# First stage of a hybrid decoder layer in quarters of two feature tiles, with squares summed on TensorE

## The chip, the core and the metric

The kernel runs on one core of one Trainium2 chip. The metric is the device time of one execution in microseconds (us), given as the median of the runs shown. The other engines of the core that matter here are ScalarE (ACT in the profile's rows), VectorE (DVE), GpSimd (POOL) and SyncE (SP), which issues nearly all loads; TensorE is PE, and its weight loads are PEld.

## What is computed

One layer of a decoder for a prompt of 1024 rows and 8 samples of 4 rows, with 1024 features. Everything is float32. What the change touches is the head of the layer: the conditioning vector goes through a silu and a product with `ada_w`, which gives a shift and a scale for each feature; the rows are normalized by their mean square, scaled and shifted, and the result `h` goes through `w_in`.

```python
def _rmsnorm(x, g):
    return x * lax.rsqrt(jnp.mean(x * x, axis=-1, keepdims=True) + EPS) * g

mod = jax.nn.silu(c) @ ada_w + ada_b
sh1, sc1, gt1, sh2, sc2, gt2 = jnp.split(mod[:, None, :], 6, axis=-1)
h = _rmsnorm(x, norm1_g) * (1.0 + sc1) + sh1
u = h @ w_in        # u_x, u_g, u_q, u_k, u_v, u_r, u_lr, u_ga, u_gb
...                 # RG-LRU branch, chunked GLA branch, merge, w_out, SwiGLU FFN
```

## The kernel before

Features lie on the 128 partitions, so the 1024 features are 8 feature tiles, and rows lie along the free dimension. The rows go in two halves: half A is the first 512 prompt rows, half B the other 512 and the 32 sample rows. A runs through the whole layer, then B. Products are made to float32 precision from two-part operands: a weight tile or an `h` tile is split into a high part (a copy by ScalarE, `split_w` line 150, `shift` line 517) and a low part (a subtraction by VectorE, lines 151 and 518), and `gemm` issues three matmuls for a tile: high by high (line 438), high by low (439), low by high (440). Only the third needs the low part of the weight, only the second the low part of `h`.

Only `begin` of half A, lines 549 to 607, is changed, with what it hands on. In it the instructions of TensorE, ScalarE and VectorE stay in the order in which they are written (`as_written`); DMAs go in program order on SP's queue. Its steps are:

- `occupy` (line 1594): dummy matmuls of a mask or a loaded tile into a bank that nobody reads, two passes each, 8 before anything has landed, 4 later.
- `load_x` (line 521): four loads of x, two feature tiles in each. ScalarE squares each tile (lines 468, 471). VectorE adds seven of the squares up into `acc` (line 473); the eighth stays by itself.
- `norm1_sum` (line 532) and `norm` (477): `ssq_mm` (line 443) multiplies 128 rows of a sum by a column of ones, four matmuls for a tile of 512 rows, two tiles in all; `rsqrt` (line 298) is eleven small VectorE instructions; `spread` (line 449) brings the result to all partitions by TensorE and a copy `rb`.
- The conditioning of half of the features (4 tiles) in one piece: chunk 2 is the scale of tiles 0 to 3, chunk 0 the shift of tiles 0 to 3, chunks 3 and 1 the same for tiles 4 to 7. A chunk is four loads of 512 KB, 16 narrow matmuls (`ada_mul`, line 205), a copy of the result by ScalarE (`ada_row`, 211), four transposes and two to three small VectorE instructions (`ada_turn`, 216; `ada_derive`, 246).
- `scaled` (line 542) multiplies x by gain and `rb`, `shift` (line 510) adds the shift and splits into high and low.
- `lr_part` (line 620): a low-rank projection, two matmuls for a feature tile. `part`: the share of a feature tile in four projections, called early (two of q, two of k), which stay in PSUM over the whole stage.

Tiles 0 to 3 are done in this way, then the products of chunks 3 and 1 come in, and parts of tiles 0 to 3 of the third and fourth projection; tiles 4 to 7 of all four and of the low-rank projection are left to `proj_h` (line 640) and `lr` (626), which run in `branches` behind `begin`. There `qk` (line 658) also makes a product `zps` (line 669) between the second and the third early projection. The first instruction after all of that on TensorE is the first matmul of `vps` (values), and from there the order on TensorE is the same in both kernels to the end.

PSUM tiles for the conditioning, the sums and the transposes come from one pool of two banks (`ax`), small float32 tiles from a pool of six (`T`), loads of 512 KB from a pool of 17 (`S`), and the high and low weight tiles from a pool of three.

Of the kernel before, what the change touches and what calls it, by code (L numbers as in the profile page):

```python
# [21 lines left out]
NB = 8  # L22
# [12 lines left out]
def starts_of(w):  # L35
    return [min(i, w - P) for i in range(0, w, P)]
# [7 lines left out]
def bc(ap, shape):  # L44
    return ap.to_broadcast(shape)
# [8 lines left out]
def hybrid_layer(ctx, tc, I, O):  # L54
# [44 lines left out]
    def ax(name):  # L99
        return axp.tile([P, 512], F32, tag="ax", name=name)  # L100
# [110 lines left out]
    def ada_row(cc, ps):  # L211
        row = T(f"adar{cc}")
        act.activation(row[:, :512], ps, AF.Copy)
        return row

    def ada_turn(cc, row):
        tps = ax(f"adat{cc}")
        for i in range(4):
            pe.transpose(tps[:, i * P:(i + 1) * P], row[:, i * P:(i + 1) * P], ident)
        mo = mod[:, 4 * cc:4 * cc + 4, :]  # L220
        dve.tensor_reduce(mo, groups(tps, 9), axis=AX.X, op=OP.add)
        dve.scalar_tensor_tensor(mo, mo, 0.5, bc(vec[:, V_ADAB + 4 * cc:V_ADAB + 4 * cc + 4].unsqueeze(2), [P, 4, 9]),
                                 op0=OP.mult, op1=OP.add)
        ada_derive(cc, mo)
# [21 lines left out]
    def ada_derive(cc, mo):  # L246
        ch, j = cc // 2, 4 * (cc % 2)
        if ch in (1, 4):
            g0 = (V_N1 if ch == 1 else V_N2) + j
            dve.scalar_tensor_tensor(gains[:, ch // 4, j:j + 4, :], mo, 1.0, bc(vec[:, g0:g0 + 4].unsqueeze(2), [P, 4, 9]),  # L250
                                     op0=OP.add, op1=OP.mult)
        if ch in (0, 3):
            sl = shd[:, ch // 3, j:j + 4, :]
            dve.tensor_sub(sl, mo[:, :, 1:9], bc(mo[:, :, 0:1], [P, 4, NB]))
        if ch in (2, 5):
            dve.tensor_scalar_mul(gains[:, 2 if ch == 2 else 3, j:j + 4, :], mo, 0.5)

    ada_next = []

# [52 lines left out]
    def drain(g):  # L312
        for _ in g:
            pass
# [74 lines left out]
    class Half:  # L389
# [159 lines left out]
        def begin(s):  # L549

            begin = len(traced())
            occupy(rmask, 8)
            s.load_x()
            a2, a0 = ada_loads(2), ada_loads(0)
            s.lr_raw = S("lr_raw")[:, :1024]
            sp.dma_start(s.lr_raw, I["w_lr"])
            ts = (T_Q, T_Q + 1, T_K, T_K + 1)
            raws = [load_raw(I["w_in"][t], 1024, f"early{t}") for t in ts[:2]]
            a3, a1 = ada_loads(3), ada_loads(1)
            raws += [load_raw(I["w_in"][t], 1024, f"early{t}") for t in ts[2:]]  # L560
            sums = s.norm1_sum()
            next(sums)
            row = ada_row(2, ada_all(2, a2))
            drain(sums)
            ada_turn(2, row)
            xns = s.scaled(range(4))
            ps = ada_all(0, a0)
            s.lr_weights()
            row = ada_row(0, ps)
            occupy(a0[3], 1)  # L570
            ada_turn(0, row)
            occupy(a0[3], 3)
            s.h = []
# [5 lines left out]
            def part(i, kt):  # L579
                s.gemm(ps[i], hl[i], 1, s.h, kt, kt == 0, False, hk=kt)  # L580

            for kt in range(4):
                s.shift(s.h, xns[kt], s.whole, kt, 0, "1" + s.n)
                if kt == 0:
                    weights(0)
                s.lr_part(kt)
                part(0, kt)
            weights(1)
            for kt in range(4):
                part(1, kt)  # L590
            row3 = ada_row(3, ada_all(3, a3))
            weights(2)
            p1 = ada_all(1, a1)
            ada_turn(3, row3)
            row1 = ada_row(1, p1)
            weights(3)
            xns = s.scaled(range(4, 8))
            for kt in range(4):
                part(2, kt)
                if kt == 1:  # L600
                    ada_turn(1, row1)
            for kt in range(4):
                part(3, kt)
            s.early = {t: (ps[i], hl[i]) for i, t in enumerate(ts)}
            for kt in range(4, 8):
                s.shift(s.h, xns[kt], s.whole, kt, 0, "1" + s.n)
            as_written(begin, (mybir.EngineType.PE, mybir.EngineType.Activation, mybir.EngineType.DVE))


# [16 lines left out]
        def lr(s):  # L626
            n = s.n
            if s.hf:
                s.lr_weights()
            for kt in range(4 * (1 - s.hf), KD):  # L630
                s.lr_part(kt)
# [962 lines left out]
    def occupy(src, n):  # L1594
        for _ in range(n):
            pe.matmul(idle, src[:, :P], src[:, :512], start=True, stop=True, skip_group_check=True)
# [17 lines left out]
    p0, p1 = B.halves  # L1614
# [111 lines left out]
```

## Time and profile before

| | us |
|---|---|
| median of 3 runs | 1978.03 |
| the three runs | 1972.02, 1978.03, 1979.07 |
| the profiled execution: its own time | 1973.25 |
| its span | 1971.5 |
| first matmul on real `h` (low-rank, line 623) | 26.18 |
| first matmul of the values (`vps`) | 59.32 |

The span runs from the first to the last instruction, the time of an execution is 1.75 longer. A timeline row gives the start, the time it took, the engine, the line, the operation, output and inputs, how many such instructions stand together, and in brackets the idle time of the engine ahead of it with what ended it. A float32 matmul of two passes stands there as two instructions. A matmul's time goes from its start to the modelled end of its result, so that matmuls in a row overlap; the step from one to the next is the distance of their starts.

### The profile page before, as it was taken

The numbers are of one execution on the slowest core, as the hardware profiler recorded it, in microseconds if no ns is written. First come the engines' busy times: TensorE is split into PE (matmuls) and PEld (weight loads), VectorE is DVE, ScalarE is ACT, GpSimd is POOL, SyncE is SP. The second block draws the span as 40 slices with busy tenths as digits, with TensorE's granted clock in tenths as the row PEclk, the third lists the DMA queues.
The fourth block names the chain that finished last, engine by engine and source line by source line (L and its number), as shares of the span: only waits on it lengthen the run. The fifth ranks groups of instructions, "written<-read, shape, count | busy, mean of one in ns | idle before, by whom it ended". The sixth has DMA issues, their size and how long they took to land. (4 is left out here: it accounts for less than half of the span.)

```text
span 1971.5 us, 33688 instructions
## 1 busy us (share of the span) xinstructions
PE 1935.8 (98%) x13428; PEld 1761.6 (89%) x13428; DVE 1319.9 (67%) x2293; ACT 944.0 (48%) x1442; POOL 107.7 (5%) x231
## 2 busy tenths in 40 slices
PE   8999999999999999999999999999999999999998
PEld 5877877776899998998899998999999999999997
DVE  5648487655548774677564597684355688888867
ACT  4645475533235452555353355563232344566653
POOL 0000001000000000000000001110222000000000
PEclk9999999999999999999999999999999999999999
DMA  8324235567544467554432323323456544556553
GB/s 339 101 103 166 70 107 200 184 228 258 206 164 155 139 189 249 176 178 141 145 102 69 133 63 100 103 88 107 134 187 223 200 141 126 173 170 183 171 163 109
DMA packets 116798, 307.68 MB, mean 156 GB/s; under 512 B 13729, under 2 KB 28833, under 8 KB 116641
## 3 DMA queue, kind: packets, MB, share of 16 engines
q1 hardware_dynamic: 104656, 260.74, 40.7%
q0 software_dynamic: 11440, 44.23, 6.2%
q8 instruction: 105, 1.72, 0.4%
q10 hardware_dynamic: 544, 0.56, 0.1%
q14 instruction: 53, 0.43, 0.1%
HBM read 271.08 MB, written 34.39 MB: 155 GB/s over the span
## 5 line engine op out<-in xcount | busy, mean ns | idle before, releaser
L151 DVE TENSOR_TENSOR fwa_hl<-fwa,fwa_hl 128x1024 fp32r<-128x1024 f32 (+1 forms) x57 | 68.8, 1206 | 44.7 <-ACT fwa_hl L150 40.8
L151 DVE TENSOR_TENSOR fwb_hl<-fwb,fwb_hl 128x1024 fp32r<-128x1024 f32 (+1 forms) x64 | 77.2, 1206 | 27.8 <-ACT fwb_hl L150 27.0
L150 ACT ACTIVATE fwa_hl<-fwa 128x1024 fp32r<-128x1024 f32 (+1 forms) x57 | 59.3, 1040 | 43.9 <-PE fapsa L1338 10.8
L150 ACT ACTIVATE fwb_hl<-fwb 128x1024 fp32r<-128x1024 f32 (+1 forms) x64 | 66.6, 1041 | 23.5 <-PE fcpsb L1338 9.1
L438 PE MATMUL f3psa<-faa,f3a_hl 128*128 128x512 f32 x176 | 68.6, 390 | 0.6 <-ACT f3a_hl L150 0.6
L440 PE MATMUL f3psa<-faa,f3a_hl 128*128 128x512 f32 x176 | 68.5, 390 | 0.4 <-DVE f3a_hl L151 0.4
L439 PE MATMUL f3psa<-faa,f3a_hl 128*128 128x512 f32 x176 | 68.6, 390 | 0.0
L150 ACT ACTIVATE f3a_hl<-f3a_raw 128x768 fp32r<-128x768 f32 (+1 forms) x32 | 25.3, 792 | 55.7 <-PE f3psa L440 47.4
L438 PE MATMUL uxpsb<-h1b,uxpsb_hl 128*128 128x256 f32 (+1 forms) x160 | 48.1, 300 | 0.1
L439 PE MATMUL uxpsb<-h1b,uxpsb_hl 128*128 128x256 f32 (+1 forms) x160 | 46.8, 292 | 0.0
L440 PE MATMUL uxpsb<-h1b,uxpsb_hl 128*128 128x256 f32 (+1 forms) x160 | 46.3, 290 | 0.0
L438 PE MATMUL ugpsb<-h1b,ugpsb_hl 128*128 128x272 f32 x160 | 46.2, 289 | 0.0
L440 PE MATMUL ugpsb<-h1b,ugpsb_hl 128*128 128x272 f32 x160 | 46.0, 288 | 0.0
L439 PE MATMUL ugpsb<-h1b,ugpsb_hl 128*128 128x272 f32 x160 | 45.8, 286 | 0.0
L438 PEld LDWEIGHTS f3psa<-faa,f3a_hl 128*128 128x128 f32 x176 | 33.0, 188 | 7.7 <-ACT f3a_hl L150 1.0
L440 PEld LDWEIGHTS f3psa<-faa,f3a_hl 128*128 128x128 f32 x176 | 33.0, 188 | 7.7 <-DVE f3a_hl L151 0.9
L151 DVE TENSOR_TENSOR f3a_hl<-f3a_raw,f3a_hl 128x768 fp32r<-128x768 f32 (+1 forms) x32 | 28.2, 888 | 16.8 <-ACT f3a_hl L150 16.6
L439 PEld LDWEIGHTS f3psa<-faa,f3a_hl 128*128 128x128 f32 x176 | 33.0, 188 | 6.8
L438 PE MATMUL wopsb<-mb,wob_hl 128*128 128x272 f32 x128 | 36.9, 289 | 1.1 <-DVE gab L1203 1.1
L438 PE MATMUL rpsb<-h1b,rpsb_hl 128*128 128x272 f32 x128 | 37.8, 295 | 0.0
L438 PE MATMUL vpsb<-h1b,vpsb_hl 128*128 128x272 f32 x128 | 37.4, 292 | 0.0
L439 PE MATMUL rpsb<-h1b,rpsb_hl 128*128 128x272 f32 x128 | 37.4, 292 | 0.0
(1131 smaller groups left out, 7739.7 us busy)
## 6 DMA issues: line engine op xcount, KB each, us to landing
ada<-in_ada_w SPq DMA_DIRECT2D x48, 512.0 KB, 6.2
fwb<-wsum SPq DMA_DIRECT2D x72, 256.0 KB, 3.4
s_raw<-in_ffn SPq DMA_DIRECT2D x32, 512.0 KB, 4.1
wsum<-s_raw POOLq DMA_DIRECT2D x32, 512.0 KB, 3.5
fwa<-wsum SPq DMA_DIRECT2D x64, 256.0 KB, 3.3
fwb<-in_ffn SPq DMA_DIRECT2D x54, 256.0 KB, 3.4
fwa<-in_ffn SPq DMA_DIRECT2D x48, 256.0 KB, 3.2
woa_raw<-in_w_out SPq DMA_DIRECT2D x13, 512.0 KB, 3.3
```

Source lines behind the costliest of these rows:

```text
L150: act.activation(hl[:, 0, :n], raw[:, :n], AF.Copy)
L151: dve.tensor_sub(hl[:, 1, :n], raw[:, :n], hl[:, 0, :n].bitcast(F32))
L438: pe.matmul(out, wh, x[:, o:o + w], start=st, stop=False)
L439: pe.matmul(out, wh, x[:, N + o:N + o + w], start=False, stop=False)
L440: pe.matmul(out, wl, x[:, o:o + w], start=False, stop=en)
```

## The change

`begin` is written anew in four quarters of two feature tiles. The loads of conditioning come in eight pairs (scale of the quarter, then its shift), each quarter's pairs followed by one of the early weights. `products` and `turn` handle half a chunk: 8 matmuls, a copy 256 wide, two transposes, and the small VectorE instructions on two tiles; `ada_derive` takes a start and a length for that. The squares aren't added on VectorE: `ssq_mm` runs on each of the eight squares as it is, 32 matmuls of one column in place of 8, on TensorE behind 5 dummy matmuls in place of 8. In the middle one dummy matmul is left of four. All four early projections and the low-rank projection are finished inside `begin`, so `proj_h` only returns the sums and `lr` has no matmuls left for half A.

```diff
-            occupy(rmask, 8)
-            s.load_x()
+            occupy(rmask, 5)
...
+            for i in range(4):
+                for c, u in cond(i):
+                    loads[c, u] = [ada_load(c, 2 * u + k) for k in range(2)]
+                if i == 0:
+                    s.lr_raw = S("lr_raw")[:, :1024]
+                    sp.dma_start(s.lr_raw, I["w_lr"])
+                raws.append(load_raw(I["w_in"][ts[i]], 1024, f"early{ts[i]}"))
...
+            for kt in range(KD):
+                sq = T(f"sq1{s.n}{kt}")
+                act.activation(sq[:, :N], s.xs[kt], AF.Square)
+                s.ssq_mm(nps, sq, starts, 0, kt == 0, kt == KD - 1)
...
+            products(*sh)
+            scale(0)
+            turn(*sh)
+            occupy(loads[sh][1], 1)
+            s.lr_weights()
+            shift(0)
+            weights(0)
+            low(0)
+            for i in range(1, 4):
+                sc, sh = cond(i)
+                k0, k1 = 2 * i - 2, 2 * i - 1
+                products(*sc)
+                part(0, k0, k1)
+                turn(*sc)
+                scale(i)
+                products(*sh)
+                for e in range(1, i):
+                    part(e, k0, k1)
+                turn(*sh)
+                weights(i)
+                part(i, *range(k1 + 1))
+                shift(i)
+                low(i)
+            for e in range(4):
+                part(e, 6, 7)
...
             if t in s.early:
-                ps, hl = s.early.pop(t)
-                s.gemm(ps, hl, 4, s.h, 4, False, True, hk=4)
-                return ps
+                return s.early.pop(t)
```

**TensorE up to the first matmul on real `h`.** Before, from the eight dummies on (`nps1a` is the sum of squares, `adaps` the products of a chunk, `rps1a` the spread, `adat` the transposes, `lrpsa` the low-rank projection):

```order
L1596 MATMUL idle<-rmask 128x512 x8
L445 MATMUL nps1a<-ones,acc1a 128x1 x4
L445 MATMUL nps1a<-ones,sq1a_181 128x1 x4
L208 MATMUL adaps_248<-ada_183,cth 32x256 x4
L208 MATMUL adaps_248<-ada_185,cth 32x256 x4
L208 MATMUL adaps_248<-ada_187,cth 32x256 x4
L208 MATMUL adaps_248<-ada_189,cth 32x256 x4
L457 MATMUL rps1a<-ident,rstd1a 128x128 x4
L219 MATMUL adat_274<-ident,adar_265 128x128 x4
```

In the changed kernel, from the seventh of eight such sums on (five dummies and six sums of four matmuls stand ahead of it):

```order
L445 MATMUL nps1a<-ones,sq1a_237 128x1 x4
L445 MATMUL nps1a<-ones,sq1a_243 128x1 x4
L584 MATMUL adaps_253<-ada_158,cth 32x256 x4
L584 MATMUL adaps_253<-ada_160,cth 32x256 x4
L592 MATMUL adat_278<-ident,adar_262 128x128 x2
L457 MATMUL rps1a<-ident,rstd1a 128x128 x4
L584 MATMUL adaps_291<-ada_162,cth 32x256 x4
L584 MATMUL adaps_291<-ada_164,cth 32x256 x4
L592 MATMUL adat_306<-ident,adar_300 128x128 x2
L1640 MATMUL idle<-ada_164 128x512
L669 MATMUL lrpsa<-h1a_317,lr_hla 128x512
L670 MATMUL lrpsa<-h1a_317,lr_hla 128x512
```

The sum of squares on TensorE is four times as long, and everything up to the low-rank projection stands behind it.

**VectorE where the second half or quarter of the conditioning arrives.** Before, at the third and fourth early weights (`xn1a` is the scaled x, `h1a` the tile `h`, whose low part is made here):

```order
L221 TENSOR_REDUCE mod<-adat_418 128x36
L222 SCALAR_TENSOR_TENSOR mod<-mod,vec 128x36
L250 SCALAR_TENSOR_TENSOR gains<-mod,vec 128x36
L169 TENSOR_TENSOR early_lo<-early_raw,early_hi 128x1024
L546 SCALAR_TENSOR_TENSOR xn1a_432<-xa_158,gains,rb1a 128x512
```

In the changed kernel, in the second quarter:

```order
L595 TENSOR_REDUCE mod<-adat_347 128x18
L596 SCALAR_TENSOR_TENSOR mod<-mod,vec 128x18
L250 SCALAR_TENSOR_TENSOR gains<-mod,vec 128x18
L546 SCALAR_TENSOR_TENSOR xn1a_353<-xa_152,gains,rb1a 128x512
L546 SCALAR_TENSOR_TENSOR xn1a_355<-xa_152,gains,rb1a 128x512
L595 TENSOR_REDUCE mod<-adat_368 128x18
L596 SCALAR_TENSOR_TENSOR mod<-mod,vec 128x18
L254 TENSOR_TENSOR shd<-mod 128x16
L151 TENSOR_TENSOR early_hl<-early_raw,early_hl 128x1024
L518 SCALAR_TENSOR_TENSOR h1a_383<-xn1a_353,mod,h1a_383 128x512
```

The low part of the quarter's weight (line 151) now stands behind the quarter's shift, which itself waits for transposes on TensorE.

**TensorE at the end of the early projections.** Before (`early_326` to `early_328` are the second to the fourth projection, `zpsa` the product of `qk`):

```order
L440 MATMUL early_326<-h1a_481,early_hl 128x512
L669 MATMUL zpsa_563<-lrta,wa_114 128x512
L669 MATMUL zpsa_566<-lrta,wa_114 128x512
L439 MATMUL early_327<-h1a_472,early_hl 128x512
L440 MATMUL early_327<-h1a_472,early_hl 128x512
```

In the changed kernel:

```order
L439 MATMUL early_252<-h1a_549,early_hi 128x512
L440 MATMUL early_252<-h1a_549,early_lo 128x512
L713 MATMUL zpsa_627<-lrta,wa_114 128x512
L713 MATMUL zpsa_630<-lrta,wa_114 128x512
L438 MATMUL vpsa_644<-h1a_317,vpsa_hl 128x512
```

The product `zps` has moved behind all of the early projections, to directly ahead of the values.

More of the change, by code (lines that the diff above doesn't have):

```diff
@@ L562, in begin @@
[L562 to L573, printed above, removed]
+            N = s.N
+            occupy(rmask, 5)
+            s.xs = []
+            for i in range(4):
+                xt = S(f"x{s.n}{i}")
+                sp.dma_start(xt[:, :2 * N], I["x" + s.n][:, i * 2 * N:(i + 1) * 2 * N])
+                s.xs += [xt[:, :N], xt[:, N:2 * N]]
@@ new lines, in begin @@
+            ts = (T_Q, T_Q + 1, T_K, T_K + 1)
+            cond = lambda i: [(c, i % 2) for c in ((2, 0) if i < 2 else (3, 1))]
+            loads, raws = {}, []
+            for i in range(4):
+                for c, u in cond(i):
[4 more added lines that the diff above has]
+                raws.append(load_raw(I["w_in"][ts[i]], 1024, f"early{ts[i]}"))
@@ new lines, in begin, with products @@
+            starts = starts_of(N)
+            nt = len(starts)
+            nps = ax("nps1" + s.n)
+            for kt in range(KD):
+                sq = T(f"sq1{s.n}{kt}")
+                act.activation(sq[:, :N], s.xs[kt], AF.Square)
+                s.ssq_mm(nps, sq, starts, 0, kt == 0, kt == KD - 1)
+            rows, xns = {}, {}
+            def products(c, u):
+                ps = ax(f"adaps{c}{u}")
+                for k in range(2):
+                    for g in range(4):
+                        pe.matmul(ps[32 * g:32 * g + 32, :256], cth[:, 4 * k + g, :], loads[c, u][k][:, g * 256:(g + 1) * 256],
+                                  start=(k == 0), stop=(k == 1), skip_group_check=True)
+                rows[c, u] = T(f"adar{c}{u}")
+                act.activation(rows[c, u][:, :256], ps[:, :256], AF.Copy)
@@ new lines, in turn @@
+            def turn(c, u):
+                tps = ax(f"adat{c}{u}")
+                for i in range(2):
+                    pe.transpose(tps[:, i * P:(i + 1) * P], rows[c, u][:, i * P:(i + 1) * P], ident)
+                j = 4 * c + 2 * u
+                mo = mod[:, j:j + 2, :]
+                dve.tensor_reduce(mo, groups(tps[:, :256], 9), axis=AX.X, op=OP.add)
+                dve.scalar_tensor_tensor(mo, mo, 0.5, bc(vec[:, V_ADAB + j:V_ADAB + j + 2].unsqueeze(2), [P, 2, 9]),
+                                         op0=OP.mult, op1=OP.add)
+                ada_derive(c, mo, 2 * u, 2)
@@ L574, in begin, with scale @@
+            def scale(i):
+                xns.update(s.scaled((2 * i, 2 * i + 1)))
             hl, ps = [None] * 4, [mm(f"early{t}") for t in ts]
@@ L577, in weights @@
                 hl[i] = (split_w if i < 3 else split_apart)(raws[i], 1024, f"early{ts[i]}")
[L579 to L606, printed above, removed]
+            def part(i, *kts):
+                for kt in kts:
+                    s.gemm(ps[i], hl[i], 1, s.h, kt, kt == 0, kt == KD - 1, hk=kt)
@@ new lines, in shift, with low @@
+            def shift(i):
+                for kt in (2 * i, 2 * i + 1):
+                    s.shift(s.h, xns[kt], s.whole, kt, 0, "1" + s.n)
+            def low(i):
+                for kt in (2 * i, 2 * i + 1):
+                    s.lr_part(kt)
+            (sc, sh) = cond(0)
+            s.h = []
+            products(*sc)
+            rstd = cp.tile([P, 5], F32, name="rstd1" + s.n, tag="rstd", bufs=2)
+            rsqrt(rstd[:, :nt], nps[:, :nt], nt, 1.0 / D, "1" + s.n)
+            turn(*sc)
@@ new lines, in begin @@
+            s.rb1 = [s.spread(rstd[:, :nt], N, "1" + s.n)]
+            products(*sh)
[9 more added lines that the diff above has]
+                k0, k1 = 2 * i - 2, 2 * i - 1
+                products(*sc)
+                part(0, k0, k1)
+                turn(*sc)
+                scale(i)
[7 more added lines that the diff above has]
+                low(i)
@@ L607, in begin @@
+            for e in range(4):
+                part(e, 6, 7)
+            s.early = dict(zip(ts, ps))
             as_written(begin, (mybir.EngineType.PE, mybir.EngineType.Activation, mybir.EngineType.DVE))
@@ L629, in lr @@
                 s.lr_weights()
-            for kt in range(4 * (1 - s.hf), KD):
-                s.lr_part(kt)
+                for kt in range(KD):
+                    s.lr_part(kt)
             ps = s.lr_ps
```

19 lines of the change are left out of this document (6 added, 13 removed).

## The prediction

> **What bounds the kernel now.** I read the page first, then the table of stretches, then the timeline of the beginning, last the granted clock. The page says whose time counts:
>
> ```profile
> span 1971.5 us, 33688 instructions
> PE 1935.8 (98%) x13428; PEld 1761.6 (89%) x13428; DVE 1319.9 (67%) x2293; ACT 944.0 (48%) x1442; POOL 107.7 (5%) x231
> ```
>
> TensorE is the bound; it lacks 35.7 us of the span. The table of stretches, cut at the first matmul on real `h` and at the first of the values, says where:
>
> ```profile
> 0.00:26.15 26.15, 21.06 (x120) 10.86 (x120) 14.70 (x61) 10.47 (x17) 2.32 (x12) 1.00 0.93 353
> 26.15:59.32 33.17, 32.07 (x189) 23.97 (x187) 18.80 (x28) 16.08 (x24) 0.00 (x0) 1.00 0.65 244
> 100.00:440.00 340.00, 339.26 (x1725) 263.84 (x1722) 220.12 (x316) 177.87 (x253) 22.03 (x42) 1.00 0.43 148
> ```
>
> (Length; busy PE, PEld, DVE, ACT, POOL; clock; DMA share; GB/s.) Behind the beginning TensorE is never short of work, 0.74 us in 340. So a microsecond won or lost before the values begin, at 59.32, is one at the end, and the change is worth what it moves that point. The timeline of the first stage:
>
> ```profile
> 12.80 0.95 PE L445 MATMUL nps1a<-ones,acc1a 128*128 128x1 f32 x8
> ...
> 14.57 1.93 PE L208 MATMUL adaps<-ada,cth 128*32 128x256 f32 x32
> 14.68 0.16 DVE L302 TENSOR_SCALAR rs_1a<-nps1a 128x4 f32<-128x4 f32 x1 [2.13 <-PE nps1a L445]
> ...
> 16.65 0.16 DVE L309 SCALAR_TENSOR_TENSOR rstd1a<-rs_1a 128x4 f32<-128x4 f32 x1
> 16.92 1.13 PE L457 MATMUL rps1a<-ident,rstd1a 128*128 128x128 f32 x8 [0.41 <-PE adaps L208]
> 17.88 0.60 PE L219 MATMUL adat<-ident,adar 128*128 128x128 f32 x4
> 18.08 0.60 ACT L460 ACTIVATE rb1a<-rps1a 128x512 f32<-128x512 f32 x1 [0.91 <-PE rps1a L457]
> ...
> 20.57 0.64 PE L208 MATMUL adaps<-ada,cth 128*32 128x256 f32 x8 [0.34 <-DMA ada<-in_ada_w]
> 21.91 1.06 ACT L616 ACTIVATE lr_hla<-lr_raw 128x1024 fp32r<-128x1024 f32 x1 [3.23 <-DMA lr_raw<-in_w_lr]
> 24.00 2.74 PE L1596 MATMUL idle<-ada 128*128 128x512 f32 x6
> 24.77 0.72 ACT L517 ACTIVATE h1a<-xn1a,mod 128x512 fp32r<-128x512 f32 x1 [1.32 <-DVE mod L222]
> 26.18 0.80 PE L623 MATMUL lrpsa<-h1a,lr_hla 128*128 128x512 f32 x1
> ```
>
> The loads end last: shift products wait until 20.57, low-rank weights until 21.91, and `h` follows. The sum of squares was known at 14.6 and its spread at 18.7.
>
> **The change, part by part.** *Loads.* The first shift products need 8 loads of 512 KB where they needed 12. At 353 GB/s or more a load takes 1.3 to 1.5 us (524 KB over that), so they land 5 us earlier, near 15.5. Loads stop being last. For the later quarters the same bytes come in another order: a quarter's five loads take 7 us, less than the 9 to 10 that a quarter will take below. On SP's queue the last load of the fourth quarter's pairs waits for the low-rank weights' buffer, free near 25; behind it stand the fourth early weight and loads for the values, needed far later, so nothing. GpSimd's one load in this stretch has nothing behind it either.
>
> *The sum of squares* is what is late next. VectorE loses six additions, but nobody waited for VectorE there. TensorE gets 64 passes of one column where it had 16. Those 16 took from 12.80 to 14.57, 0.11 each, so 64 take 7.0. They start behind 5 dummies, six passes fewer at 0.43 (six take 2.74, of which the last about 0.6), at 12.8 - 2.6 = 10.2, and end at 17.3, not 14.6. Two squares now wait for a buffer of the six; TensorE comes to them only at 15, so that costs nothing. The root takes 14.68 to 16.81, 2.1: 19.5. The spread and its copy took 1.9: 21.4, not 18.7.
>
> *First shift.* Its products stand behind the spread's passes, from 20.6: 16 passes at 0.05 (31 steps in 1.93 less a last one of 0.38) end at 21.8. A copy of 256 columns is not in the trace; between a small instruction (0.2) and the 512 columns of `rb` (0.60) I take 0.4: 22.2. Two transposes 0.4, the dummy 1.0: 23.6. The low-rank weights take the buffer that this dummy reads, so ScalarE waits for it: 1.06 and 0.7 for the tile make 25.4 for the first real matmul, 0.8 earlier than 26.18.
>
> *The four quarters.* The prices:
>
> ```profile
> 24.20 0.31 DVE L221 TENSOR_REDUCE mod<-adat 128x36 f32<-128x144 f32 x1 [0.91 <-PE adat L219]
> ...
> 24.77 0.19 DVE L254 TENSOR_TENSOR shd<-mod 128x32 f32<-128x32 f32 x1
> 25.40 1.04 ACT L150 ACTIVATE early_hl<-early_raw 128x1024 fp32r<-128x1024 f32 x1
> ...
> 38.35 1.23 DVE L151 TENSOR_TENSOR early_hl<-early_raw,early_hl 128x1024 fp32r<-128x1024 f32 x1 [7.53 <-ACT early_hl L150]
> ...
> 39.63 0.50 PE L440 MATMUL early<-h1a,early_hl 128*128 128x512 f32 x1 [0.37 <-DVE early_hl L151]
> ...
> 59.32 0.39 PE L438 MATMUL vpsa<-h1a,vpsa_hl 128*128 128x512 f32 x1
> ...
> 64.53 0.39 PE L440 MATMUL vpsa<-h1a,vpsa_hl 128*128 128x512 f32 x1
> ```
>
> A wide matmul takes 0.2265 (24 from 59.32 to 64.53, 23 steps). From the first real matmul on TensorE has 112 of them in either kernel, 25.4; narrow passes 64 before, 96 now (5.0); transposes 8, now 12 (1.3); two `zps` 0.45. That is 32.1 of work, where it was 30.1, since half of the first scale and shift no longer lies ahead. Stalls before: 33.1 - 30.1 = 3.0.
>
> Stalls now: in each later quarter the low part of the new weight stands on VectorE behind the shift. After the transposes: 0.2 for their result, 0.7 for three small instructions, 1.23 for the low part, 2.2 in all; TensorE has 0.7 to do meanwhile (a transpose and two matmuls). 1.5 to 1.7, three times. In the second quarter nothing stands between the shift's products and its transposes either, so their copy (0.8) and ScalarE's split of the weight behind it (1.04, of which 0.8 shows) come on top, and the third matmul's wait is 1.2 there. With the ramp of the first two tiles, 0.6 to 0.8, and small change: 0.8 + 2.7 + 1.6 + 1.7 = 6.8. The values begin at 25.4 + 32.1 + 6.8 = 64.3, 5.0 late.
>
> *The product `zps`*, moved behind everything, puts the scores' chain later against the values:
>
> ```profile
> 54.33 1.26 ACT L653 ACTIVATE za<-zpsa,vec 128x512 f32<-128x512 f32 x2
> ...
> 57.71 1.22 DVE L726 SCALAR_TENSOR_TENSOR ea<-za 128x1024 f32<-128x1024 f32 x1
> ...
> 72.69 1.22 DVE L151 TENSOR_TENSOR vpsa_hl<-vpsa_raw,vpsa_hl 128x1024 fp32r<-128x1024 f32 x1
> ...
> 78.80 0.69 PE L830 MATMUL spsa<-wa 128*64 128x64 f32 x16 [0.29 <-ACT vfa L712]
> ```
>
> Its copy ended at 55.6, 3.7 ahead of the values, and will end 1.3 behind: 5.0. Of that the chain waited 2.1 for VectorE (to 57.7), which will be free then, and 1.2 lay in it for a value weight (72.69) that stands ahead now: 5.0 - 2.1 - 1.2 = 1.7 at the scores, which wait already. A copy of k that stood in it on ScalarE (0.6) is done ahead too, which leaves 1.1. Bounds 0 and 3.7, I take 1.2.
>
> *The clock.* One-column passes are the open price: do they keep the clock up? Two places where it fell (the last fence gives the one-column passes `opsb` of its stretch alone):
>
> ```profile
> 445.79:449.21 3.42, 0.00 (x0) 0.00 (x0) 2.87 (x5) 0.00 (x0) 0.53 (x1) 1.00 0.72 277
> 449.21:452.62 3.41, 2.22 (x8) 1.94 (x9) 2.27 (x6) 2.81 (x5) 0.53 (x1) 0.50 0.96 335
> 452.62:456.03 3.41, 3.41 (x15) 1.83 (x13) 1.60 (x5) 1.95 (x2) 0.00 (x0) 0.50 0.96 330
> 456.03:459.44 3.41, 3.41 (x18) 2.71 (x15) 3.41 (x7) 1.34 (x2) 1.33 (x2) 1.00 0.93 292
> ```
>
> ```profile
> 1261.58:1264.99 3.41, 2.92 (x22) 2.67 (x22) 2.60 (x7) 2.27 (x4) 0.00 (x0) 1.00 0.64 222
> 1264.99:1268.40 3.41, 3.41 (x13) 2.95 (x12) 2.68 (x10) 2.21 (x4) 0.00 (x0) 0.50 0.13 39
> ```
>
> ```profile
> 1261.58:1264.99 3.41, 1.98 (x17) 1.81 (x16) 0.17 (x1) 1.00 0.64 222
> ```
>
> It fell to half behind 3.4 us without work, and also behind 3.4 us in which TensorE was busy for 2.92, but 1.98 of that with one-column passes. It came back behind a stretch that was full, not behind one that was 65% full. In the change 10.2 to 17.3 is one-column passes and nothing else, two such stretches long, so wherever the steps of 3.41 lie the clock falls between 13.6 and 17.1. Then passes take double:
>
> ```profile
> 450.40 1.12 PE L219 MATMUL adat<-ident,adar 128*128 128x128 f32 x4 [4.82 <-ACT adar L213]
> ...
> 452.17 0.63 PE L438 MATMUL pbpsa<-yba,pba_hl 128*128 128x512 f32 x1
> ...
> 454.73 0.63 PE L438 MATMUL pbpsa<-yba,pba_hl 128*128 128x512 f32 x1
> ```
>
> (1.12 for the 0.60 of four transposes; wide 0.43, six steps in 2.56.) With a fall at 15.7: the rest of the sum +1.6; spread +0.9, products +0.9, transposes and dummy +1.2. The first real matmul is 4.6 late, at 30. Up to the first full stretch, some 3 to 6 us on, half of the busy time is lost, 1 to 2.5. Together 5.5 to 7, I take 6.0.
>
> The Trainium skill, "TensorE: Matmul & The Clock Gate", section "Why this matters for your kernels", asks only that TensorE have no idle gap over some 3 us between bursts. By that rule the clock would stay up here, for no gap comes near that, and the sum would be 6.2 in place of 12.2. The rows of 1261.58 differ: there TensorE idles 0.49 in all, and the clock falls.
>
> **Sum.** 5.0 + 1.2 + 6.0 = 12.2 us later. The profiled execution took 1973.25, so 1985.5 in its terms. It lies in the low half of the runs shown (1972.02 to 1979.07); the four executions have a mean of 1975.6, and 1975.6 + 12.2 makes 1988. Half a percent, 9.9 us, is about what a measurement of this kernel can tell from no change.
>
> **Rivals.** *The clock stays up*: the sum of squares keeps TensorE busy by the engine's own count, as between 12.3 and 14.6 before, and only stalls and work remain. 5.0 + 1.2 = 6.2, 1982. For it: the clock column is 1.00 through the whole first stage before. Against it: that stretch also held dummies and narrow products.
>
> *The quarters run without a hole*, on the other side: the clock stays up, and TensorE's queue has the row copies and low parts in time, because ScalarE and VectorE are little used there (16.08 and 18.80 of 33.17). The first real matmul at 25.4, 32.1 of work and the first ramp 0.6 make 58.1, 1.2 early; with the scores' chain as before, 1974. It is decided at the third matmul of a quarter's new projection: if the low part is there when TensorE arrives, this holds. Against it: that part is behind the shift in VectorE's order. No more than this can be won: the load, the sum of squares and the work set 58.
>
> *The clock stays down*: every quarter has a stall of over a microsecond, so no stretch is full until the long run of the fourth projection. The second and third quarter then take some 5 us more, 17 in all, 1993.
>
> **How the numbers follow.** Forecast 0.62, the clock stays up 0.20, without a hole 0.08, the clock stays down 0.10. The range takes in the last (1993 and, from the upper runs, 1997) and the lower end of the case with the clock up (6.2 less the 3 that its stalls and the scores are uncertain by, from the mean: 1978; the third reaches lower, and with a part of it I set 1977). Slower by over half a percent: nearly three quarters of the forecast (12.2 with some 3 either way against 9.9) and the whole of the last case, 0.54. Faster by as much would need 9.9 and the bound is 1.2: 0.03, for the measurement. Within: 0.43.
>
> **What would show it.** Right: 64 one-column passes from about 10.2 to beyond 17; the root's first instruction past 17.3; a granted clock of 0.5 from some 15 to past 30; the first real matmul near 30; waits of 1.2 to 1.7 of the third matmul of the second to fourth projection on VectorE's low part; values from 69 to 71; a wait of 1 to 2 at the scores. With the clock at 1.00 throughout, values at 64 and the first rival holds. Values before 60 would make the whole walk wrong; so would a part of the loss given back behind them, in a place where TensorE has idle time now.

## The result, and the profile of the changed kernel

| | before | changed |
|---|---|---|
| median of 7 runs each, us | 1973.68 (1966.12 to 1979.07) | 1985.35 (1983.00 to 1987.26) |
| span of the profiled execution | 1971.5 | 1985.5 |
| first matmul on real `h` | 26.18 | 27.91 |
| first matmul of the values | 59.32 | 70.68 |

The ratio is 1.0055, with a 95% interval from 1.0041 to 1.0069: 8 to 14 us slower, 11 in the middle. The forecast was 12.2 slower, 1988 in a range from 1977 to 1997.

The page of the changed kernel, the same two lines as before:

```profile
span 1985.5 us, 33781 instructions
PE 1944.0 (98%) x13464; PEld 1769.8 (89%) x13464; DVE 1319.5 (66%) x2299; ACT 943.5 (48%) x1446; POOL 108.3 (5%) x231
```

The table of stretches, cut at the same two events (length; busy PE, PEld, DVE, ACT, POOL; granted clock; DMA share; GB/s), and behind the first three rows five steps of 3.41 us:

```profile
0.00:27.91 27.91, 22.18 (x120) 16.00 (x120) 9.55 (x53) 9.35 (x17) 1.76 (x11) 0.82 0.94 352
27.91:70.68 42.77, 37.90 (x222) 25.36 (x223) 21.90 (x41) 15.73 (x25) 0.55 (x1) 0.96 0.45 164
100.00:440.00 340.00, 339.67 (x1737) 263.84 (x1736) 220.63 (x320) 180.42 (x259) 20.72 (x39) 1.00 0.43 145
9.21:12.62 3.41, 3.41 (x32) 3.41 (x33) 0.00 (x0) 2.30 (x4) 0.00 (x0) 1.00 1.03 418
12.62:16.04 3.42, 3.42 (x18) 3.42 (x18) 0.00 (x0) 0.00 (x0) 0.00 (x0) 0.50 1.03 418
19.45:22.86 3.41, 2.85 (x20) 1.89 (x13) 1.82 (x11) 0.38 (x1) 0.00 (x0) 0.50 1.03 410
26.27:29.69 3.42, 1.49 (x4) 0.67 (x4) 1.94 (x4) 3.15 (x4) 0.00 (x0) 1.00 1.02 407
29.69:33.10 3.41, 3.41 (x20) 1.76 (x20) 0.99 (x1) 0.38 (x1) 0.55 (x1) 0.50 1.02 405
```

The first stage is 1.7 us longer, the second 9.6 (42.77 for 33.14). In the 340 us of the third row TensorE idles for 0.33, where it idled for 0.74 before: a wait of 0.5 for a load (`adaps`) is gone, and so little is given back. The clock is 0.82 in the first stage and 0.96 in the second, 1.00 in both before. It is half from 12.62 to 22.86 and again from 29.69 to 33.10. The step ahead of the first fall is the plainest row: TensorE busy for all 3.41 us, 32 passes, and half clock behind it.

The timeline of TensorE up to the first real matmuls, and the places where it waits later:

```profile
8.69 10.06 PE L445 MATMUL nps1a<-ones,sq1a 128*128 128x1 f32 x64
18.67 1.93 PE L584 MATMUL adaps<-ada,cth 128*32 128x256 f32 x16
...
21.65 1.64 PE L457 MATMUL rps1a<-ident,rstd1a 128*128 128x128 f32 x8
23.22 1.07 PE L584 MATMUL adaps<-ada,cth 128*32 128x256 f32 x16
24.85 0.44 PE L592 MATMUL adat<-ident,adar 128*128 128x128 f32 x2 [0.56 <-ACT adar L587]
25.13 1.02 PE L1640 MATMUL idle<-ada 128*128 128x512 f32 x2
27.91 0.49 PE L669 MATMUL lrpsa<-h1a,lr_hla 128*128 128x512 f32 x1 [1.76 <-ACT h1a L517]
...
38.09 0.50 PE L440 MATMUL early<-h1a,early_hl 128*128 128x512 f32 x1 [0.72 <-DVE early_hl L151]
...
47.72 0.50 PE L440 MATMUL early<-h1a,early_hl 128*128 128x512 f32 x1 [1.41 <-DVE early_hl L151]
...
60.11 0.50 PE L440 MATMUL early<-h1a,early_lo 128*128 128x512 f32 x1 [1.44 <-DVE early_lo L169]
...
84.70 0.63 PE L731 MATMUL vtpa<-ident,vfa 128*128 128x128 f32 x4 [1.18 <-DVE atta L801]
```

The sum of squares is one block of 64 passes in 10.06 us and the root starts when it ends. In the first 110 us no matmul waits for a load any more. The third matmul of a new projection waits for VectorE's low part in each later quarter. The last row is a wait that the kernel before did not have: the first transposes of the values, 14 us behind their first matmul.

### The profile page after: what moved, and what is told of

It reads as the page before. It is cut to its first block, busy times and chain, and to the rows that moved or that the text cites. A ratio compares the mean times of both kernels' runs of the same rounds, so it can differ in the third digit from the quotient of the medians.

```text
span 1985.5 us, 33781 instructions
## 1 busy us (share of the span) xinstructions
PE 1944.0 (98%) x13464; PEld 1769.8 (89%) x13464; DVE 1319.5 (66%) x2299; ACT 943.5 (48%) x1446; POOL 108.3 (5%) x231
## 5 line engine op out<-in xcount | busy, mean ns | idle before, releaser
L438 PE MATMUL wopsb<-mb,wob_hl 128*128 128x272 f32 x128 | 37.7, 295 | 2.4 <-DVE gab L1247 2.4
L438 PE MATMUL rpsb<-h1b,rpsb_hl 128*128 128x272 f32 x128 | 37.8, 295 | 0.0
L440 PE MATMUL wopsb<-mb,wob_hl 128*128 128x272 f32 x128 | 37.6, 294 | 0.0
```

What stands on the lines that cost most here:

```text
L438: pe.matmul(out, wh, x[:, o:o + w], start=st, stop=False)
L440: pe.matmul(out, wl, x[:, o:o + w], start=False, stop=en)
```

## The experiments

Eleven kernels were run. "Half clock" is the time up to 100 us in which the trace's clock records show 0.50; the ratio is to the kernel before, run beside them on the same chip (medians of 1971.34, 1972.29 and 1971.61 in the three groups). Line numbers in rows are those of each kernel itself.

| kernel | first real matmul | values | half clock | ratio, 95% interval |
|---|---|---|---|---|
| before | 26.18 | 59.32 | 0 | |
| changed | 27.91 | 70.68 | 13.7 | 1.0055 [1.0041, 1.0069] |
| squares added on VectorE | 23.91 | 65.15 | 3.4 | 1.0049 [1.0032, 1.0065] |
| before, with the tile sums alone | 29.61 | 62.57 | 6.8 | 1.0015 [1.0006, 1.0024] |
| weights first | 28.51 | 65.55 | 10.2 | 1.0047 [1.0032, 1.0061] |
| wide passes between the sums | 32.91 | 76.49 | 17.1 | 1.0080 [1.0067, 1.0094] |
| place of `zps` | 27.89 | 70.43 | 10.2 | 1.0059 [1.0036, 1.0082] |
| three parts put back | 23.72 | 60.77 | 3.4 | 1.0017 [1.0001, 1.0032] |
| sums 64 columns wide | 24.38 | 67.15 | 3.4 | 1.0051 [1.0032, 1.0070] |
| all parts | 22.66 | 61.40 | 6.8 | 1.0002 [0.9988, 1.0016] |
| all parts, three dummies | 22.96 | 59.23 | 0 | 1.0011 [1.0000, 1.0022] |
| wide sums, weights, `zps` | 24.38 | 61.45 | 0 | 1.0009 [0.9996, 1.0023] |
| sums 16 columns wide | 28.22 | 71.02 | 13.7 | one run: 1984.31 us |

The whole times follow the values only roughly. With the squares on VectorE, with the weights first and with the wide sums the values come 5.5, 5.1 and 3.5 us earlier than in the changed kernel, and by the ratios the whole times are 1.2, 1.6 and 0.8 us shorter, with intervals of some 3 us either way. The steps at half clock behind 440 us lie partly elsewhere in their traces; that they make the difference is not shown. So what a part costs is read at the values, and the whole time is used where parts are put together.

The theory was that of the prediction: the one-column passes bring the clock down, and that costs about as much as all the rest. The rival: length of the sum, waits and work explain the loss, and the clock matters little.

**Squares added on VectorE.** One part of the change undone.

```diff
-            occupy(rmask, 5)
+            occupy(rmask, 8)
...
-            for kt in range(KD):
-                sq = T(f"sq1{s.n}{kt}")
-                act.activation(sq[:, :N], s.xs[kt], AF.Square)
-                s.ssq_mm(nps, sq, starts, 0, kt == 0, kt == KD - 1)
+            acc = [ACC("1" + s.n)]
+            for kt in range(KD):
+                s.add_sq(acc, s.xs[kt], N, kt, f"1{s.n}{kt}", True)
+            for i, a in enumerate(acc):
+                s.ssq_mm(nps, a, starts, 0, i == 0, i == len(acc) - 1)
```

> The changed kernel with its squares added up on VectorE as before (eight dummies, 16 one-column passes in place of 64); quarters, loads and zps as changed. Theory, the clock: the 64 one-column passes bring it to half from 12.6 to 22.9 and leave so little behind them that it falls again from 29.7 to 33.1. Then here the granted clock is full from the dummies to 100 us, the sum ends near 14.6, the first real matmul is at 22.5 to 24.5 (27.91 with the change), the values begin at 61.5 to 64 (70.68), and the time is 7 to 9 us under the changed kernel's, 2 to 4 us over the kernel before (ratio 1.001 to 1.002). Rival, work and stalls alone: only the shorter sum is won, 2.6 us, and the clock still falls in the waits ahead of the first real matmul: values at 67 to 68, 3 us under the changed kernel's time.

The table of stretches of this kernel, one step and the second stage:

```profile
16.39:19.80 3.41, 3.03 (x21) 2.32 (x24) 1.02 (x6) 0.60 (x1) 0.00 (x0) 0.50 1.01 405
23.91:65.15 41.24, 36.36 (x222) 24.69 (x223) 21.91 (x41) 15.73 (x25) 0.55 (x1) 1.00 0.56 209
```

The first real matmul came where the theory had it, but the clock still fell for one step, and the values are 1.2 us later than its bound. The gain of 5.53 at the values lies between the two theories (7 to 9, and 3). The second row says where the theory was off: at full clock throughout, the second stage takes 41.24, and the forecast had 38.9. The time, 9.7 us over the kernel before (6.3 to 12.8), misses the 2 to 4 of the theory and fits the rival's, which was some 8. In the profiled execution the 5.8 by which the values are late have become 9.1 at the end of the span (1980.6 for 1971.5); where the rest comes from stays open.

**Before, with the tile sums alone.**

```diff
-            occupy(rmask, 8)
+            occupy(rmask, 5)
...
             for kt in range(KD):
-                s.add_sq(s.acc, s.xs[kt], N, kt, f"1{s.n}{kt}", s.hf == 0)
+                if s.hf == 0:
+                    sq = T(f"sq1{s.n}{kt}")
+                    act.activation(sq[:, :N], s.xs[kt], AF.Square)
+                    s.acc.append(sq)
+                else:
+                    s.add_sq(s.acc, s.xs[kt], N, kt, f"1{s.n}{kt}")
```

> The kernel before with nothing but its squares summed tile by tile on TensorE (64 one-column passes behind five dummies). Theory, the clock: half from 12.6 to at least 19.4, first real matmul at 28 to 30 (26.18 before), values at 61.5 to 64.5 (59.32), time 2 to 5 us over the kernel before. Rival, length alone: the sum ends at 17.3 and the conditioning, which ended last, hides nearly all of it: first real matmul at 26.5 to 27, values at 59.5 to 60.5, time within 1 us of before.

Its stretches, two steps of its sum of squares:

```profile
11.87:15.29 3.42, 3.42 (x32) 3.42 (x33) 0.00 (x0) 0.63 (x1) 0.00 (x0) 1.00 1.03 419
15.29:18.70 3.41, 3.41 (x18) 3.41 (x17) 0.00 (x0) 0.00 (x0) 0.00 (x0) 0.50 1.03 411
```

As the theory had it: the clock falls behind the first step that holds nothing but one-column passes, the values are 3.25 late, and the time is 3.0 us longer (1.2 to 4.7). In the other kernel, with no quarters, the passes have the same effect, so they cause the fall and not the new order.

**Weights first.** In each quarter the weight is split at the quarter's start.

```diff
             shift(0)
-            weights(0)
...
+                weights(i)
                 products(*sc)
                 part(0, k0, k1)
...
                 turn(*sh)
-                weights(i)
```

(The first quarter's `weights(0)` goes ahead of the spread.)

> The changed kernel with each quarter's early weight split at the quarter's start, ahead of its conditioning on ScalarE and VectorE; the sum as changed. Theory, the low parts behind the shift cost 0.72, 1.41 and 1.44 us and the high part 0.51: these waits of the projections go, values at 66.5 to 68 (70.68), time 3 to 4 us under the changed kernel's; the clock falls at 12.6 as before. Rival, the wait only changes its place: the split (1.04 on ScalarE, 1.23 on VectorE) now stands ahead of the row copies and small instructions, so the transposes wait for ScalarE and the products of h for the shift: values at 69.5 to 71, time as the changed kernel's.

The second stage of this kernel:

```profile
28.51:65.55 37.04, 35.95 (x222) 24.82 (x223) 21.20 (x40) 14.79 (x24) 0.55 (x1) 1.00 0.49 182
```

The four waits are gone, and only one of 0.3 has come in their place (for a low part of `h`): the stage is 37.04, against 41.24 in the run above, 4.20 for waits of 0.51, 0.72, 1.41 and 1.44, which add to 4.08. The values are even 5.1 earlier than with the change, more than expected, since the second fall of the clock is gone too. The time, 9.3 us over the kernel before (6.3 to 12.0), does not show the gain of 3 to 4 that was expected in it.

**Wide passes between the sums.**

```diff
                 s.ssq_mm(nps, sq, starts, 0, kt == 0, kt == KD - 1)
+                if kt % 2:
+                    occupy(rmask, 1)
```

> The changed kernel with one wide dummy matmul (two passes, 0.86 us) behind every second square's sums, four in all, so 3.4 us more work for TensorE in the sum. Theory, the clock is what is lost: wide passes are a third of the time in the sum, so the clock stays full; the sum ends near 19 as it does at half clock, what follows runs at full clock, first real matmul at 26.5 to 27.5 (27.91), values at 66.5 to 68.5 (70.68), time 2 to 4 us under the changed kernel's although it does more. Rival, the length of TensorE's work sets it: 3.4 us more ahead of the root, values at 73 to 74, time 2 to 4 us over the changed kernel's.

Its stretches:

```profile
8.68:18.92 10.24, 10.24 (x67) 7.93 (x65) 0.39 (x3) 2.40 (x4) 0.00 (x0) 1.00 1.03 415
18.92:29.16 10.24, 9.68 (x53) 5.40 (x52) 3.40 (x16) 0.98 (x2) 0.00 (x0) 0.50 1.03 408
29.16:32.57 3.41, 1.43 (x8) 0.47 (x4) 1.28 (x5) 1.77 (x3) 0.00 (x0) 1.00 1.02 407
32.57:39.40 6.83, 6.49 (x25) 3.51 (x26) 2.64 (x3) 2.23 (x4) 0.55 (x1) 0.50 1.04 397
```

Both expectations failed. The clock stayed up for the first three steps, and then it fell all the same, for 17.1 us in all, so this kernel paid for the dummies and for the clock: values 5.8 later than with the change. That a third of the time in wide passes would do was my estimate, and it was too little: in the step ahead of the fall, from 15.50 to 18.92, only two wide passes begin (`idle` in the timeline), in the step ahead of that one three. The run tells the theories apart no further.

**Place of `zps`.** The last two feature tiles of the third and fourth projection go back to the branch code.

```diff
-            for e in range(4):
+            for e in range(2):
                 part(e, 6, 7)
-            s.early = dict(zip(ts, ps))
+            s.early = {t: (ps[i], hl[i], i) for i, t in enumerate(ts)}
...
-                return s.early.pop(t)
+                ps, hl, i = s.early.pop(t)
+                if i > 1:
+                    s.gemm(ps, hl, 2, s.h, 6, False, True, hk=6)
+                return ps
```

> The changed kernel with the last two feature tiles of the third and fourth early projection left to the branch code, as in the kernel before, so that zps stands 24 wide matmuls ahead of the values' end of the queue less what the first two take; all else as changed. Theory, zps behind everything delays the scans and with them the release of a PSUM bank on VectorE: with the change the first values' transposes wait 1.18 us for that and the scores no longer wait (0.29 before). Here the transposes wait 0 to 0.2 again, the scores 0 to 0.4, the values begin where they did, within 0.5 us for equal clock, and 0.8 to 1.2 us are won. Rival, the scans are late because the whole stage is: the wait of 1.2 stays, and nothing is won.

The table of waits of TensorE in the first 110 us, for this kernel (the changed one has 1.2 for `vtpa` there, and no wait for `h` at line 438):

```profile
PE early L438 <- ACT h1a L517: 0.8, 1, 0.8
...
PE vtpa L734 <- DVE atta L804: 0.5, 1, 0.5
```

The wait of the transposes is 0.7 shorter but not gone; 0 to 0.2 was expected. With fewer matmuls left at the end, one of them waited for the last `h` (the 0.8, new). By the time of the later scores this kernel is 0.9 ahead of the changed one, of which 0.25 lay at the values already (it also has one step less at half clock), so the place is worth 0.7 behind the values; the whole time cannot show so little.

**Three parts put back.** The edits of the first, third and fifth run together.

> The changed kernel with three parts put back together: squares added on VectorE, each quarter's weight split at the quarter's start, zps ahead of the last parts. Theory, the three terms add: of the 11.4 us at the values the sum with its clock is 5.5, the waits for the low parts 3.6 to 4.1, and the transposes' wait is 0.9 to 1.2 behind them: values at 60.5 to 61.5 (70.68 with the change, 59.32 before), transposes' wait under 0.3, time 1 to 3 us over the kernel before. Rival, they overlap, since a shorter first part only brings other waits forward: values at 62.5 to 65, time 4 to 7 us over.

Its second stage:

```profile
23.72:60.77 37.05, 35.96 (x223) 24.83 (x223) 21.01 (x40) 15.37 (x25) 0.56 (x1) 1.00 0.61 233
```

The terms add: values at 60.77, the transposes' wait 0.2, the time 3.4 us over the kernel before (0.2 to 6.3). The rival of overlapping terms is out.

**Sums 64 columns wide.** The clean test of the clock: as many passes with the same weights, only more equal columns in each.

```diff
-                s.ssq_mm(nps, sq, starts, 0, kt == 0, kt == KD - 1)
+                for i, o in enumerate(starts):
+                    pe.matmul(nps[:, 64 * i:64 * i + 64], sq[:, o:o + P], rmask[:, 1:65],
+                              start=(kt == 0 and i == 0), stop=(kt == KD - 1 and i == len(starts) - 1), skip_group_check=True)
```

(`rmask` is one in these columns; the root reads every 64th column.)

> The changed kernel with 64 equal columns in place of one in each pass of its sum of squares; as many passes, the same squares, nothing else touched. Theory, a pass takes its time from the load of its 128 columns of weights, and the clock goes by the columns that stream: passes still take about 0.11 us, but the clock stays full, the sum ends 3 us earlier (64 passes in 7 us, not 10), the first real matmul is at 24 to 25 (27.91), and without a second fall the values begin at 65 to 67 (70.68), time 4 to 6 us under the changed kernel's. Rival, the clock goes by how long TensorE is occupied or waits: half from about 12.6 as with one column, values at 70 to 71. Second rival, wider passes are longer: the clock stays full but the sum takes 10 us or more, values at 68 to 70.

The stretch of the sum, the second stage and a later step of this kernel, and its first real matmul:

```profile
9.06:16.24 7.18, 7.18 (x65) 7.11 (x63) 0.00 (x0) 2.40 (x4) 0.00 (x0) 1.00 1.03 417
24.38:67.15 42.77, 37.91 (x223) 25.43 (x223) 21.91 (x41) 15.74 (x25) 0.56 (x1) 0.96 0.53 197
33.84:37.25 3.41, 3.41 (x18) 1.90 (x20) 0.47 (x1) 0.00 (x0) 0.00 (x0) 0.50 1.02 405
```

```profile
24.38 0.50 PE L671 MATMUL lrpsa<-h1a,lr_hla 128*128 128x512 f32 x1 [1.76 <-ACT h1a L517]
```

The 64 passes take 7.18 us at full clock, 0.11 each, in place of 10.06, and the clock stays up through the whole first stage. The values come 3.53 earlier. The first fall is thereby shown to come from how few columns stream, not from how long TensorE is occupied, and priced at the values: 3.5 us. A fall for one step remains, in the second quarter behind its waits, so the values miss the expected 65 to 67 by a little, and the second stage is 42.77, to the hundredth what it was with the change. The whole time does not show the gain: it is 10.1 us over the kernel before (6.3 to 13.8), where 4 to 6 under the changed kernel's 10.9 was expected.

**All parts.** The run of three, 64 columns in the 16 passes of its sum, and in the first quarter:

```diff
-            s.lr_weights()
             shift(0)
-            low(0)
+            s.lr_weights()
+            part(0, 0)
```

(`low(0)` follows the next scale's products, `part(0, 1)` its shift's products.)

> The three parts of the run before put together, and two more: 64 columns in each of the 16 passes of the sum, and in the first quarter the shift and the early projection ahead of the low-rank weights and their matmuls. Theory, what is left against the kernel before is half the clock in one window (about 1 us) and 1.1 us of ScalarE's split of the low-rank weights ahead of the first h: values at 58.3 to 59.8 (59.32 before, 60.5 to 61.5 in the run of three), time within 2 us of the kernel before. Rival, the work of six separate narrow products and transposes is what is left and other waits fill in: values at 60.5 or later, time 1 to 3 us over.

Its stretch behind the dummy, and its first real matmul:

```profile
22.23:29.06 6.83, 6.40 (x29) 3.17 (x33) 2.99 (x5) 3.38 (x5) 0.56 (x1) 0.50 1.02 407
```

```profile
22.66 0.80 PE L438 MATMUL early<-h1a,early_hl 128*128 128x512 f32 x1 [1.64 <-ACT h1a L517]
```

The expectation failed at the values, 61.40: the first real matmul is 1.1 earlier, but it falls into two steps at half clock behind narrow products and a wait of 1.64. The whole time is 0.4 us over the kernel before (-2.4 to 3.2), as expected.

**All parts, three dummies.**

```diff
-            occupy(loads[sh][1], 1)
+            occupy(loads[sh][1], 3)
```

> The run with all parts put together (values at 61.40, granted clock half from 22.23 to 29.06 behind a wait of 1.64 us for the first h), with three wide dummies in place of one ahead of that wait; two take 1.7 us, as long as the wait. Theory, that half clock is what lay between its 61.40 and the 58.3 to 59.8 expected: the clock stays full, the wait goes into the dummies, values at 58.3 to 59.8, and 1.5 to 3 us are won against that run. Rival, the dummies only stand in the way: the first real matmul is over 1 us later and the values are at 60.5 or later.

Both stages of this kernel, cut near the first real matmul and the values:

```profile
0.00:22.50 22.50, 17.97 (x82) 9.27 (x82) 13.73 (x58) 8.76 (x16) 1.76 (x11) 1.00 0.91 344
22.50:59.20 36.70, 36.13 (x224) 24.82 (x223) 21.21 (x41) 16.58 (x27) 0.55 (x1) 1.00 0.66 249
```

The clock stays full, the first real matmul is 0.3 later (22.96), and the values come 2.17 earlier, at 59.23, as the theory had it and where they stood in the kernel before (59.32). In whole time it is 2.2 us over that kernel (0 to 4.3), no gain on the run without the dummies that the intervals could show.

**Wide sums, weights, `zps`.** The edits of the third, fifth and seventh run together.

> The changed kernel with the squares still summed on TensorE, but 64 equal columns wide, and with the weights split at the quarter's start and zps ahead of the last parts. Theory, of the sum on TensorE only its one-column form was dear: first real matmul at 24 to 25 as with the wide sums alone (23.72 with VectorE's sum), then the 37.05 us of the run of three: values at 61 to 62.2 (60.77), time within 2 us of that run. Rival, squares on TensorE cost by their number: values at 63.5 or later.

```profile
24.38:61.45 37.07, 35.99 (x223) 24.82 (x223) 21.00 (x40) 15.29 (x25) 0.55 (x1) 1.00 0.59 226
```

That is its second stage, 37.07. With the clock up, squares on TensorE end 0.7 us behind squares on VectorE at the values (61.45 and 60.77), though the latter also had one step at half clock. The number of passes was a small matter, their one column a large one.

**Sums 16 columns wide.** The same edit with 16 for 64.

> The changed kernel with 16 equal columns in place of one in each pass of its sum of squares. Theory, the clock goes by the share of time in which columns stream; with 16 in a pass that is an eighth or less: the clock falls to half in the sum as with one column, the sum takes 9.5 to 10.5 us, the first real matmul is at 27 to 28.5. Rival, any pass of more than one column keeps it up: the sum takes 7.0 to 7.5 us and the first real matmul is at 24 to 25.

Its sum in the timeline, and two stretches:

```profile
8.97 9.82 PE L577 MATMUL nps1a<-rmask,sq1a 128*128 128x16 f32 x64
```

```profile
9.79:13.20 3.41, 3.41 (x33) 3.41 (x32) 0.00 (x0) 1.42 (x3) 0.00 (x0) 1.00 1.02 416
13.20:23.44 10.24, 9.68 (x53) 8.19 (x52) 2.38 (x14) 0.38 (x1) 0.00 (x0) 0.50 1.03 412
```

Sixteen columns behave like one: the clock falls behind the first step of such passes, the values are at 71.02.

## Why the prediction was right, step by step

The sum of the forecast came out for two reasons: its mechanisms were there, and, by luck, the errors in the sizes of its terms nearly cancel. The work was forecast 2.3 too low, the first matmul 1.0 too late and the clock 0.9 too dear. Measured with the clock up (first real matmul from the wide sums, second stage from VectorE's sums), the terms are:

| term | forecast | measured | from |
|---|---|---|---|
| first real matmul, clock full | -0.8 | -1.8 | 24.38 - 26.18 |
| second stage: waits | +3.8 | +3.8 | 4.8 - 1.0, by the tables of waits |
| second stage: work | +2.0 | +4.3 | 41.24 - 33.14 - 3.8 |
| clock | +6.0 | +5.1 | 3.53 and 42.77 - 41.24 |
| values, in all | +11.0 | +11.4 | 70.68 - 59.32 |
| behind the values | +1.2 | +1.0 | 104.5 - 92.1 at the first of the later scores, less 11.4 |

*Loads* stop being last: right. The root waits for the sum and the first real matmul for ScalarE, as the timeline shows.

*The sum of squares.* 64 passes by 0.11: right at full clock, 7.18 measured for 7.0. In the wide sums it started at 9.06 and not at 10.2, and that is most of the 1.0 by which the first term was off. This was luck: the first dummies stand 0.85 us apart and the later ones 0.43, and the switch came later in the profiled execution of the kernel before. Its first ten dummy passes took 7.4 us (2.85 to 10.23), and the ten of the wide sums 6.2 (2.85 to 9.06).

*First shift.* The copy of 256 columns takes 0.38, forecast 0.4; the wait for the low-rank weights behind the dummy is 1.76, forecast 1.06 and 0.7. Right.

*The four quarters.* The tables of waits of TensorE in the second stage, of the kernel before and then of that with the squares on VectorE, whose clock is full there:

```profile
PE lrpsa L623 <- ACT h1a L517: 0.6, 1, 0.6
PE early L440 <- DVE early_hl L151: 0.4, 1, 0.4
```

```profile
PE early L440 <- DVE early_hl L151: 2.1, 2, 1.4
...
PE early L440 <- DVE early_lo L169: 1.4, 1, 1.4
PE early L438 <- ACT early_hl L150: 0.5, 1, 0.5
PE adat L593 <- ACT adar L588: 0.5, 1, 0.5
PE lrpsa L671 <- DVE h1a L518: 0.3, 1, 0.3
```

1.0 before and 4.8 now, so the difference is 3.8, as forecast. Each side was taken 2.0 too high, though, 3.0 and 6.8: what the forecast called stalls before was what its prices of work left over, and it set the second quarter at 2.7 and the ramp at 0.8, which took 1.7 and 0.3. The mechanism is right: the third matmul of a new projection waits 0.72, 1.41 and 1.44 where 1.2 and twice 1.5 to 1.7 were forecast, on VectorE's low part as said, and the run with the weights first takes these waits away. The step that failed in size is the work. The changed kernel's timeline, third quarter:

```profile
40.13 1.07 PE L584 MATMUL adaps<-ada,cth 128*32 128x256 f32 x16
41.13 0.50 PE L438 MATMUL early<-h1a,early_hl 128*128 128x512 f32 x1
41.47 0.40 PE L439 MATMUL early<-h1a,early_hl 128*128 128x512 f32 x1
...
42.65 0.38 PE L592 MATMUL adat<-ident,adar 128*128 128x128 f32 x2
42.96 1.07 PE L584 MATMUL adaps<-ada,cth 128*32 128x256 f32 x16
```

A group of 16 narrow passes takes 1.00 from start to next, not 16 by 0.052; the first wide matmul behind it takes 0.34, not 0.2265; two transposes take 0.31, not 0.22. That is 0.37 a group, and 2.2 for six groups, nearly all that was missing. I took the step inside a long run and multiplied it, and the quarters cut the run into short groups, each with a changeover to pay.

*The clock.* It fell because of the one-column passes: right, shown by 64 columns in their place. When was less right. It fell at 12.62, forecast 13.6 to 17.1, and came back at 22.86, forecast 33 to 36: the step ahead of that was not full, TensorE was busy for 2.85 of its 3.41 us. And it fell a second time, which was not forecast, behind a step with the wait for the first real matmul in it, busy for 1.49 of 3.42. So the first real matmul was at 27.91 and not near 30: the first fall cost 3.5 there, forecast 4.6, and the second cost 1.5 in the second stage, where 1 to 2.5 was forecast for the end of the one fall. In all 5.1 for 6.0.

The Trainium skill, "TensorE: Matmul & The Clock Gate", section "Why this matters for your kernels", puts the loss of clock down to gaps of more than some 3 us without work. The row 9.21:12.62 disagrees, with no gap at all and half clock behind it. By that rule the first rival would have held, 6.2 in place of 12.2.

*`zps`.* Right in size, wrong in place. The scores do not wait; the first transposes of the values do, 1.18 us for VectorE's read `atta` of the products `dpsa`. VectorE's rows of the two kernels, before and then changed:

```profile
70.35 1.29 DVE L757 TENSOR_TENSOR atta<-dpsa,ident 128x512 f32<-128x512 f32 x2
```

```profile
83.87 1.29 DVE L801 TENSOR_TENSOR atta<-dpsa,ident 128x512 f32<-128x512 f32 x2
```

The read comes 13.2 behind the first value matmul, 11.0 before: 2.2 later, because it stands behind the scans of `za` in VectorE's order (they begin at 78.01, 64.24 before). I followed the chain to its end and not to what it held up on its way.

The rivals: the clock did not stay up; the quarters were not without a hole; and the clock did not stay down until the fourth projection. In the medians the loss is 11.7.

The profiled execution is 12.4 late at the later scores and 14.0 at the end of its span, and the way between is not level. At the last of the scores (`spsa`, 216.3 us in the kernel before) it is 11.8 late, and at a product of the other half (`posb`, 1253.9) 10.9: TensorE, coming later, no longer waits 0.5 for a load of conditioning (`adaps`), and waits 0.2 in place of 1.0 for the load that `posb` reads. So a little of the loss is given back at waits for loads, which the prediction had named as a sign against its walk; it is small, 1.5, and does not touch the terms above. Behind that 3.1 are lost, at a wait of 2.4 for 1.1 in the merge and one more step at half clock, from 1555.45 to 1558.86. Some of the other kernels have such a step there (weights first, wide sums), some have not (place of `zps`, three parts put back); whether it belongs to the change stays open.

No version beat the kernel before. With the faults named here mended the values start at 59.23 for 59.32. The first real matmul is 3.2 earlier than before (22.96 for 26.18) and the second stage 3.1 longer (36.27 for 33.14): the narrow products and transposes that moved into it, 2.0 by the forecast, and the 2.2 that their short groups add cost about what the earlier start and the shorter waits give.

## What to carry to other kernels

A stretch in which TensorE is busy can still bring its clock down: look at the columns that stream, and where a reduction needs one column, let it carry 64 equal ones if the time of a pass does not change (16 were too few here). When work is cut into smaller groups, price a group from a row of that size, with its changeover to the next shape, not from the step inside a long run. When something moves later in an engine's order, follow not only its result but each thing queued behind it, down to who waits for a buffer.

## What the runs showed of the hardware

A pass with 128 weight columns takes 0.11 us with 1 column as with 64 (16 in 1.8 us before, 64 in 7.18 with 64 columns): the extra columns are free here. With 1 and with 16 columns the clock falls, with 64 it stays.

The spread between executions of one kernel goes with the granted clock. Over 64 runs of the kernel before the time follows the mean granted clock: 1965.8 to 1970.7 us in nine runs at 0.997, 1974.6 to 1978.5 in four at 0.993. One step of 3.41 us at half clock is 0.0009 of the mean and, worked out, costs at most 1.7 us, half its length; from 0.997 to 0.993 are four to five such steps, up to 8 us, and the two groups lie some 8 us apart. That the steps make the spread is argued from this, not shown by a run.
